# Storing a pooling state in contiguous rows after a copy on the chip, in a hybrid decoder step

## The chip, the core and the metric

The kernel runs on one core of a Trainium2 chip, as one program. The metric is device time in microseconds: the median of three runs. The core has five engines that run side by side and wait for one another through semaphores: PE (matrix products), DVE (VectorE), ACT (ScalarE), POOL (GpSimd) and SP (SyncE, which here only issues transfers). ACT and POOL can issue transfers too. In the profile, "SPq" and "ACTq" are the issues of transfers by SP and ACT.

## What is computed

One inference step of two layers for a prompt of 1024 positions and a group of 8 samples that share the weights. Layer 0 mixes a multi-scale pooling branch with an RWKV-7 branch; layer 1 is a chunked gMLP. Each layer then has cross-attention into 256 memory tokens and a squared-ReLU MLP. What matters here is the state that the pooling branch hands on: for each sample, the last 15 of the rows (15 old ones, then the new one).

```python
def pool_mix(z, buf, pos0, w_group, scale):
    full = jnp.concatenate([buf.astype(z.dtype), z], axis=1)
...
    return y.astype(z.dtype), full[:, -POOL_BUF:]
```

`buf` is `state_pool`, 8 samples x 15 rows x 512 channels in float32; the second result is `pool_sample`, of the same shape. The kernel keeps channels in partitions (128 channels x 4 groups), so on the chip and in its output tensor `ps` the state is 128 rows of 480 numbers: 4 groups x 8 samples x 15 rows.

## The kernel before

**Arithmetic.** The large products are made in float32 from three products of a high and a low part. A weight unit (128 x 1024) is loaded by SP into one of two buffers `wr` (L204, in `wunit`), its high part is cast by ACT (L194), and its low part is formed by DVE or POOL (L195). PE then runs three products per block (L225, L226, L227, in `mm3`). A buffer `wr` can be loaded again when both parts of its earlier unit are made.

**Order.** The program is written once as straight code, and the build fixes an order of instructions for each engine and each issuing queue from its own estimate of when each is ready. This order is not the written one: in the profile SP issues L969 and L970, which are written after the loop over the four pooling groups, ahead of the third group's L967. On the chip each engine takes its list strictly in order, so an instruction that waits holds all that stand behind it on that engine.

**What runs around the change.** Around 375 us four pieces of work are interwoven by generators:
- `pooling()` (L931 to 972), four groups. For each: the last rows of the prompt and the new sample column are copied by POOL (L940, L941); windowed sums by doubling on POOL or DVE (L946, with small copies L947); the mean minus the token (L953 to L958); a 128 x 128 product (L965) whose result ACT scales (L966); and a store of the group's result into `mixd` by SP (L967). At the end the two pooling states are stored: the prompt's (`pp`, L969) and the samples' (`ps`, L970).
- `inverses(s)` (L893 to 914): DVE inverts small triangular blocks by a loop of L907 and L908; ACT makes a transposed copy (L911); SP stores both forms into `xid` (L912, L913).
- `indep` and `Chain` (L1117 to 1216): the chunked RWKV recurrence. For each segment ACT issues the loads of `prd` (L1124), `xid` (L1130, L1131), `abd` (L1135) and `vd` (L1137), PE works on them (L1145, L1154), and then a serial chain of small products follows (L1178 to L1212).
- `memkv` (L1025 to 1058): keys and values of the memory tokens, unit by unit from `in_wk` and `in_wv`, used to fill PE's time between the chain's steps. For each unit of keys, DVE scales the product (L1032) and SP stores it to the output `mk` (L1033).

**The names of the edit.** `pbuf` is one 128-partition buffer. Its first 512 columns, viewed as `pb4`, hold for 4 groups and 8 samples 16 entries each: the 15 old rows and the new one. Columns 512 to 991 are `pin`, into which the old state is loaded (L928), contiguous; POOL spreads it from there into `pb4` (L929), and `pin` is not read again. The state that is stored is `pb4[..., 1:16]`: 15 numbers, one left out, 15 numbers, and so on.

Of the kernel before, what the change touches and what calls it, by code (L numbers as in the profile page):

```python
# [125 lines left out]
def hybrid_step(ctx: ExitStack, tc: tile.TileContext, I, O):  # L126
    nc = tc.nc
    te, ve, se, po, sy = nc.tensor, nc.vector, nc.scalar, nc.gpsimd, nc.sync
# [13 lines left out]
    def get(dt=F32):  # L142
        i = free.popleft()
        t = sb.tile([128, T], dt, tag=f"s{i}", name=nm("s"))
        owner[id(t)] = (i, t)
        return t

    def put(*ts):
        for t in ts:
            free.append(owner.pop(id(t))[0])  # L150

    def small(shape, tag, bufs=2, dt=F32):
        return sb.tile(shape, dt, tag=tag, bufs=bufs, name=nm(tag))
# [20 lines left out]
    def psm():  # L174
        return cyc("m", ("in0", "in1", "c0b", "c1b") if wide[0] else ("in0", "in1"))
# [11 lines left out]
    def pc(name, i):  # L187
        c = PCOL[name] + i
        return par[:, c : c + 1]
# [463 lines left out]
    def bulk(n=1):  # L653
        for _ in range(n):
            next(zs_, None)
            if side and next(side[0], 0) == 0:
                side.popleft()
# [268 lines left out]
    pb4 = pbuf[:, 0:512].rearrange("p (g b t) -> p g b t", g=4, b=8)  # L926
    pin = pbuf[:, 512:992]
# [3 lines left out]
    def pooling():  # L931
        for g in range(4):
            zused[0] = zorder.index(g)
            while g not in zready:
                bulk()
                yield
            zused[0] += 1
            z = zready.pop(g)
            win = WIN[g]
            po.tensor_copy(out=ppo[:, g, :], in_=z[:, NP - 15 : NP])  # L940
            po.tensor_copy(out=pb4[:, g, :, 15:16].rearrange("p b t -> p (b t)"), in_=z[:, NP:T])  # L941
            cur, step = z, 1
            while step < win:
                nx = get()
                eng = (po, ve)[PG[{1: 0, 2: 4, 4: 8, 8: 12}[step] + g]]
                eng.tensor_tensor(out=nx[:, step:NP], in0=cur[:, step:NP], in1=cur[:, 0 : NP - step], op=ALU.add)  # L946
                po.tensor_copy(out=nx[:, 0:step], in_=cur[:, 0:step])  # L947
                if cur is not z:
                    put(cur)
                cur, step = nx, step * 2  # L950
            d = get()
            o = C1["cnt"][0] + 16 * g
            ve.scalar_tensor_tensor(out=d[:, 16:NP], in0=cur[:, 16:NP], scalar=1.0 / win, in1=z[:, 16:NP], op0=ALU.mult, op1=ALU.subtract)  # L953
            ve.tensor_tensor(out=cur[:, 0:16], in0=cur[:, 0:16], in1=c1[:, o : o + 16], op=ALU.mult)
            ve.tensor_tensor(out=d[:, 0:16], in0=cur[:, 0:16], in1=z[:, 0:16], op=ALU.subtract)
            t = small([128, 8], "pws")
            ve.tensor_reduce(out=t, in_=pb4[:, g, :, 16 - win : 16], axis=AX.X, op=ALU.add)
            ve.scalar_tensor_tensor(out=d[:, NP:T], in0=t, scalar=1.0 / win, in1=z[:, NP:T], op0=ALU.mult, op1=ALU.subtract)  # L958
            put(cur)
            bulk()  # L960
            for _ in range(PLY):
                yield
            for g0, g1 in GR:
                ps = psm()
                te.matmul(ps[:, : g1 - g0], g2t[:, 512 + g * 128 : 640 + g * 128], d[:, g0:g1], start=True, stop=True)  # L965
                se.activation(out=z[:, g0:g1], in_=ps[:, : g1 - g0], func=AF.Copy, scale=pc("psc", g))  # L966
            sy.dma_start(out=mixd[g], in_=z)  # L967
            put(z, d)
        sy.dma_start(out=O["pp"], in_=ppo)  # L969
        sy.dma_start(out=O["ps"].rearrange("p (n t) -> p n t", t=15), in_=pb4[:, :, :, 1:16].rearrange("p g b t -> p (g b) t"))  # L970
        put(pbuf, g2t, c1)
        yield

# [289 lines left out]

    segs = [[(0, n)] * (n < 4) + [(1, n - 1)] * (n > 0) for n in range(5)]
    pg = pooling()

    def start(n):
# [897 lines left out]
```

## Time and profile before

| | us |
|---|---|
| median of 3 runs (3176.22 to 3179.43) | 3179.05 |
| the profiled execution | 3185.59 |
| its span, first to last instruction | 3183.8 |
| POOL busy in it | 717.3 |
| store of `ps` (L970): issued at | 375.48 |
| store of `ps`: from issue to landing | 17.9 |
| store of `pp` (L969), 30 KB, contiguous rows: from issue to landing | 1.5 |

The profile is of one execution, and all times in it are counted from its span's start. A row of the timeline reads: start, duration, engine, line, operation, output<-inputs, shape, and in brackets the idle time of that engine just before and what ended it. A row of issues reads: what was moved, the issuing queue, how many, KB each, and the median time from issue to landing. A row of waits reads: who waited <- for whom: total us, times, the longest.

### The profile page before, as it was taken

What the parts mean: (1) busy time and instruction counts of PE and PEld (TensorE: products, weight loads), DVE (VectorE), ACT (ScalarE), POOL (GpSimd) and SP (SyncE); (2) the same over time, 40 slices, a digit from 0 to 9 for tenths busy, and PEclk for the clock granted to TensorE, in tenths of its full rate; (3) what the DMA queues carried; (4) which work ended last, traced back from release to release, by engine and by line L of the source; (5) the groups of instructions that cost most, each with busy time, mean ns of one, the idle gap of its engine ahead of it and who ended that gap; (6) DMA issues with size and microseconds to landing.
All of it is one profiled execution on the core that took longest, in us unless ns stands there. A gap on an engine that the chain in (4) does not pass through costs nothing. (4 is left out here: it accounts for less than half of the span.)

```text
span 3183.8 us, 59345 instructions
## 1 busy us (share of the span) xinstructions
PE 3081.0 (97%) x23514; PEld 2957.1 (93%) x23514; DVE 2086.6 (66%) x3778; ACT 1353.3 (43%) x2757; POOL 717.3 (23%) x650
## 2 busy tenths in 40 slices
PE   8999889999999999999999999999999999999998
PEld 7987778899899999999999999899989999999998
DVE  4688734644457887566787776656455788765775
ACT  5223234433345444544455454614334544453443
POOL 5233424320021223022131100223001122211213
PEclk9999989999999999999999999999999999999999
DMA  3346577643522444866522223524343244476643
GB/s 119 117 132 208 88 247 234 209 140 120 180 87 103 158 160 173 218 174 174 174 89 99 88 94 138 204 80 143 113 147 120 94 158 156 164 236 140 181 166 121
DMA packets 215846, 473.25 MB, mean 149 GB/s; under 512 B 47374, under 2 KB 72334, under 8 KB 215567
## 3 DMA queue, kind: packets, MB, share of 16 engines
q1 hardware_dynamic: 188814, 423.63, 39.0%
q0 software_dynamic: 6912, 25.37, 4.6%
q10 hardware_dynamic: 19840, 20.45, 2.3%
q8 instruction: 185, 3.03, 0.4%
q14 instruction: 95, 0.77, 0.1%
HBM read 309.87 MB, written 159.50 MB: 147 GB/s over the span
## 5 line engine op out<-in xcount | busy, mean ns | idle before, releaser
L454 PE MATMUL ps<-s,wp 128*128 128x258 f32 x3584 | 1018.7, 284 | 11.3 <-DVE s L490 5.9
L456 PE MATMUL ps<-s,wp 128*128 128x258 f32 x3584 | 1013.2, 283 | 4.4 <-DVE wp L195 4.2
L455 PE MATMUL ps<-s,wp 128*128 128x258 f32 x3584 | 1014.1, 283 | 0.0
L454 PEld LDWEIGHTS ps<-s,wp 128*128 128x128 f32 x3584 | 677.8, 189 | 15.2 <-DVE s L490 6.7
L456 PEld LDWEIGHTS ps<-s,wp 128*128 128x128 f32 x3584 | 678.9, 190 | 5.7 <-DVE wp L195 5.7
L455 PEld LDWEIGHTS ps<-s,wp 128*128 128x128 f32 x3584 | 680.5, 190 | 0.2 <-issue 0.2
L225 PE MATMUL ps<-s,wh 128*128 128x384 f32 (+2 forms) x1994 | 649.5, 327 | 19.3 <-ACT wh L194 16.5
L226 PE MATMUL ps<-s,wh 128*128 128x384 f32 (+2 forms) x1994 | 643.6, 323 | 0.1
L227 PE MATMUL ps<-s,wl 128*128 128x384 f32 (+2 forms) x1994 | 640.0, 322 | 0.4 <-DVE wl L195 0.4
L225 PEld LDWEIGHTS ps<-s,wh 128*128 128x128 f32 x1994 | 380.6, 191 | 30.4 <-ACT wh L194 17.3
L226 PEld LDWEIGHTS ps<-s,wh 128*128 128x128 f32 x1994 | 381.1, 191 | 7.9 <-issue 6.0
L227 PEld LDWEIGHTS ps<-s,wl 128*128 128x128 f32 x1994 | 380.0, 191 | 6.0 <-issue 4.1
L265 POOL TENSOR_TENSOR s<-s,m 128x384 f32<-128x384 f32 (+1 forms) x147 | 162.0, 1110 | 652.6 <-ACT m L264 651.7
L194 ACT CAST s<-s 128x516 fp32r<-128x516 f32 (+6 forms) x316 | 199.2, 657 | 144.2 <-DMA s<-hts 32.5
L195 DVE TENSOR_TENSOR wp<-wr,wp 128x512 fp32r<-128x512 f32 x200 | 159.9, 800 | 89.9 <-ACT wp L194 88.1
L194 ACT CAST wh<-wr 128x1024 fp32r<-128x1024 f32 x110 | 115.1, 1047 | 200.1 <-PE ps L226 155.1
L194 ACT CAST wp<-wr 128x512 fp32r<-128x512 f32 x200 | 124.5, 622 | 129.1 <-issue 48.3
L195 DVE TENSOR_TENSOR wl<-wr,wh 128x1024 fp32r<-128x1024 f32 x97 | 121.5, 1254 | 58.5 <-ACT wh L194 53.9
L195 DVE TENSOR_TENSOR s<-s,s 128x516 fp32r<-128x516 f32 (+6 forms) x148 | 122.5, 841 | 52.2 <-ACT s L194 40.5
L225 PE MATMUL ps<-s,s 128*128 128x384 f32 (+3 forms) x432 | 142.9, 333 | 6.9 <-ACT s L1768 6.5
L195 DVE TENSOR_TENSOR s<-s 128x516 fp32r<-128x516 f32 x168 | 116.3, 726 | 37.5 <-ACT s L194 37.0
L226 PE MATMUL ps<-s,s 128*128 128x384 f32 (+3 forms) x432 | 139.6, 323 | 0.0
(346 smaller groups left out, 5271.3 us busy)
## 6 DMA issues: line engine op xcount, KB each, us to landing
hdn<-s SPq DMA_DIRECT2D x128, 258.0 KB, 2.1
hts<-s SPq DMA_DIRECT2D x48, 516.0 KB, 2.7
s<-hts SPq DMA_DIRECT2D x96, 258.0 KB, 6.6
xf<-s POOLq DMA_DIRECT2D x48, 516.0 KB, 7.5
s<-hdn SPq DMA_DIRECT2D x72, 258.0 KB, 5.4
s<-in_wd SPq DMA_DIRECT2D x34, 512.0 KB, 5.2
s<-in_kc SPq DMA_DIRECT2D x64, 256.0 KB, 3.6
s<-in_vc SPq DMA_DIRECT2D x64, 256.0 KB, 3.1
```

The source lines that it names most:

```text
L194: se.copy(out=hi, in_=src)
L195: (eng or ve).tensor_tensor(out=lo, in0=src, in1=f(hi), op=ALU.subtract)
L225: te.matmul(out, wh, xh, start=i == 0, stop=False)
L226: te.matmul(out, wh, xl, start=False, stop=False)
L227: te.matmul(out, wl, xh, start=False, stop=i == n - 1)
L265: po.tensor_tensor(out=self.acc[:, g0:g1], in0=self.acc[:, g0:g1], in1=sq, op=ALU.add)
L454: te.matmul(out, wh, xh, start=j < 4 and k == 0, stop=False, skip_group_check=j >= 4)
L455: te.matmul(out, wh, xl, start=False, stop=False, skip_group_check=j >= 4)
L456: te.matmul(out, wl, xh, start=False, stop=k == 3, skip_group_check=j >= 4)
```

## The change

After the four groups, POOL copies the 480 state numbers of each partition from `pb4` (runs of 15 with one left out) into `pin`, where they lie side by side, and SP stores `pin` to the output as 128 rows of 1920 bytes. Before, SP stored straight from `pb4`, in runs of 15 numbers (60 bytes). The bytes written to the output are the same. POOL gets one instruction more, and SP's store now waits for it.

```diff
         sy.dma_start(out=O["pp"], in_=ppo)
-        sy.dma_start(out=O["ps"].rearrange("p (n t) -> p n t", t=15), in_=pb4[:, :, :, 1:16].rearrange("p g b t -> p (g b) t"))
+        po.tensor_copy(out=pin.rearrange("p (n t) -> p n t", t=15), in_=pb4[:, :, :, 1:16].rearrange("p g b t -> p (g b) t"))
+        sy.dma_start(out=O["ps"], in_=pin)
         put(pbuf, g2t, c1)
```

## The prediction

> **What bounds the kernel now.** I read the page's first part, then PE busy time by stretch around the edited line, then what PE and SyncE waited for there, then the timelines of the five engines, and last the landing times of the transfers.
>
> ```profile
> span 3183.8 us, 59345 instructions
> PE 3081.0 (97%) x23514; PEld 2957.1 (93%) x23514; DVE 2086.6 (66%) x3778; ACT 1353.3 (43%) x2757; POOL 717.3 (23%) x650
> ```
>
> PE is busy 3081.0 of 3183.8 us. A transfer can only matter if it is behind part of the 102.8 us in which PE is not. The edited store is issued at 375.48 us, so the stretches after it come next (columns: PE, PEld, DVE, ACT, POOL busy us and instructions, granted clock, DMA share, GB/s).
>
> ```profile
> 381.00:385.00 4.00, 0.00 (x0) 0.00 (x0) 4.00 (x8) 0.10 (x1) 3.56 (x4) 0.50 2.05 26
> 385.00:391.00 6.00, 5.87 (x19) 4.69 (x20) 5.58 (x16) 0.00 (x0) 1.61 (x3) 0.50 1.33 68
> 395.00:405.60 10.60, 0.00 (x0) 0.00 (x0) 0.00 (x0) 3.92 (x4) 0.00 (x0) 0.65 0.74 247
> 405.60:411.80 6.20, 6.15 (x26) 5.74 (x26) 1.56 (x2) 1.53 (x2) 0.00 (x0) 0.50 1.06 396
> ...
> PE ps L225 <- ACT wh L194: 12.4, 2, 10.9
> ...
> SPq L204 <- DMA out_mk<-m: 14.0, 1, 14.0
> ```
>
> Two holes in PE's work, 381 to 385 and 395 to 405.6, each followed by some 6 us at a granted clock of 0.50. In the first hole DVE is busy all of 4.00 us: that hole is DVE's. In the second, DVE and POOL do nothing and ACT 3.92 us: nobody computes. Its last releaser for PE is the cast of a weight unit (L194), and the weight load behind that (L204) stood 14.0 us on SyncE until a 128 KB result store, out_mk, had landed. Now the chain itself, SyncE first, then the engines.
>
> ```profile
> 375.48 0.57 SPq L970 DMA_DIRECT2D out_ps<-s  x1
> 377.11 6.14 SPq L967 DMA_DIRECT2D mixd<-s  x1
> 383.34 0.56 SPq L1033 DMA_DIRECT2D out_mk<-m  x1
> 398.00 0.33 SPq L204 DMA_DIRECT2D wr<-in_wk  x1
> ...
> 400.95 0.32 SPq L913 DMA_DIRECT2D xid<-s  x1
> ...
> 380.80 12.96 ACTq L1131 DMA_DIRECT2D s<-xid  x4
> ...
> 399.01 1.92 ACT L911 COPY s<-s 128x1024 f32<-128x1024 f32 x1
> ...
> 404.55 1.04 ACT L194 CAST wh<-wr 128x1024 fp32r<-128x1024 f32 x1 [3.15 <-DMA wr<-in_wk]
> ...
> 409.48 0.36 ACTq L1131 DMA_DIRECT2D s<-xid  x1
> ...
> 394.33 0.28 PE L226 MATMUL ps<-s,wh 128*128 128x256 f32 x1
> 394.44 0.28 PE L227 MATMUL ps<-s,wl 128*128 128x256 f32 x1
> 405.65 0.58 PE L225 MATMUL ps<-s,wh 128*128 128x256 f32 x1 [10.93 <-ACT wh L194]
> ...
> 411.88 0.64 PE L1145 MATMUL ps<-s,s 128*32 128x32 f32 x28
> ```
>
> The issue of the mixd store takes 6.14 us and that of four small xid loads 12.96 us, where the issue of the weight load at 398.00 takes 0.33. Both queues are choked from 377 to 394 us. What chokes them is in the DMA view: first the edited store, then the same kinds of transfers over the whole span, then those issued from 376 to 394 us, with that window's two queues.
>
> ```profile
> out_ps<-s SPq DMA_DIRECT2D x1, 240.0 KB, 17.9
> out_wks<-s SPq DMA_DIRECT2D x4, 256.0 KB, 2.5
> wr<-in_wk SPq DMA_DIRECT2D x16, 512.0 KB, 5.6
> s<-prd ACTq DMA_DIRECT2D x16, 512.0 KB, 4.7
> out_mk<-m SPq DMA_DIRECT2D x16, 128.0 KB, 6.2
> ...
> q1 hardware_dynamic: 4192, 0.31, 104.8%
> q10 hardware_dynamic: 496, 0.96, 44.2%
> s<-prd ACTq DMA_DIRECT2D x2, 512.0 KB, 18.0
> s<-xid ACTq DMA_DIRECT2D x4, 32.0 KB, 16.0
> out_mk<-m SPq DMA_DIRECT2D x1, 128.0 KB, 14.6
> ```
>
> The edited store moves 128 rows of 32 runs of 15 floats: 4096 runs of 60 bytes, 245,760 bytes. The window's SyncE queue (q1) shows 4192 packets for 0.31 MB, so nearly all are those runs. It lands after 17.9 us, at 393.4; the neighbours that were issued behind it take 14.6 to 18.0 us, those of ACT's queue (q10) included.
>
> **The change, part by part.** *The store.* It becomes 128 runs of 1920 bytes. The nearest row is out_wks: 256 KB from 128 contiguous rows of 2048 bytes, 2.5 us. I take 2.5 for 17.9, so 15.4 us of choked queues go. By itself that gives PE nothing; its worth is what it frees.
>
> What is late next, in order. The weight load (L204, call its unit U3) reuses the buffer of the unit before last, free when DVE has made that unit's low part:
>
> ```profile
> 385.77 1.22 DVE L195 TENSOR_TENSOR wl<-wr,wh 128x1024 fp32r<-128x1024 f32 x1
> ...
> 388.14 0.18 DVE L908 TENSOR_TENSOR s<-s,s 128x31 f32<-128x31 f32 x1
> ...
> xid<-s SPq DMA_DIRECT2D x2, 512.0 KB, 8.5
> ```
>
> DVE is in unbroken work there (4.00 of 4.00 and 5.58 of 6.00 us above), so 386.99 stays. The mixd store's issue, unchoked, ends near 377.5 instead of 383.25, so out_mk goes out between 377.5 and 383.3; I take 380 and its median of 6.2, which is before 387. (From 383.3 it would be 389.5, and U3 some 2.5 us later.) U3's load goes out at 387.0 instead of 398.0, lands 5.6 later (its median) at 392.6, is cast in 1.04 and is ready at 393.7; PE gets to it at 394.44 + 0.28 = 394.7. **The 10.93 us hole is gone**. Without it the 24 matmuls of U3 and the two of L965 do not run at half clock: 6.20 us of that stretch against 24 x 0.12 (the like matmuls at 394.33 and 394.44 start 0.11 apart, 0.12 with rounding) + 0.6 = 3.5, another **2.7**. Taken alone the two give 13.6 us, and that is the upper bound.
>
> PE then stands at 398.2 before L1145, which needs the second set of inverted blocks (xid), written by SyncE and read back by ACT. DVE finishes them at 388.32 (L908); ACT's copy (L911, 1.92) is now free to start then, as ACT no longer stands in its choked issues: 390.2. The xid store follows at 390.3. In the profile these stores took 8.5 us, in stretches at 247 and 396 GB/s; I keep that, since U3's load and ACT's abd loads (512 KB each) will move at the same time: 398.8. From the first xid load of ACT after it (409.48) to L1145 (411.88) are 2.4 us: **L1145 at 401.2 instead of 411.88, 10.7 us earlier.** So of 13.6 us, 3.0 go to a new wait.
>
> *The added copy.* The reverse of this copy, same shape, is L929:
>
> ```profile
> L929 POOL COPY s<-s x1: 583/583/583, 288.6 to 288.6; 128x480 f32<-128x480 f32 x1
> ...
> 375.11 2.86 POOL L946 TENSOR_TENSOR s<-s 128x1023 f32<-128x1023 f32 x1
> ...
> 380.76 0.94 POOL L1120 MEMSET s<- 64x1024 f32 x1 [2.54 <-PE ps L1212]
> ...
> 379.86 1.21 DVE L946 TENSOR_TENSOR s<-s 128x1022 f32<-128x1022 f32 x1
> ...
> 391.08 1.04 POOL L1226 TENSOR_TENSOR s<-s,gnq 128x512 f32<-128x512 f32 x1 [1.56 <-DVE gnq L1225]
> 424.14 1.65 POOL L1231 TENSOR_TENSOR gnq<-gnq,mhalf 128x8 f32<-128x8 f32 x1 [32.01 <-DVE gnq L1230]
> ```
>
> 0.58 us, in POOL's 2.54 us of idleness before 380.76: cost nothing. If it goes ahead of POOL's L946 instead, that addition and its small copies end 0.58 after 378.2, and DVE, which needs them at 379.86, has 1.6 us to spare: nothing again. It may be slower beside DVE (POOL's own L946 takes 2.86 us for what DVE does in 1.21); even three microseconds still leave it done by 382.
>
> *The added wait.* The store now waits for POOL, so it moves on SyncE from 375.48 to about 379. Behind it stand the mixd store, out_mk and U3's load. The first is read much later, and U3's load is not due before 387.0. Between 379 and 387 the wait costs nothing.
>
> *Carrying to the end.* After 411.8 the order on every engine is fixed, and what PE waits for is released by earlier work that has moved too (10.9 of the 12.4 us that it waits for L194 up to 600 us are this hole), so I carry the 10.7 us whole. The ends here are all of it, and half, should a later load be no earlier; I take the whole, as no row shows such a load.
>
> **Sum.** 3185.59 (profiled execution: 3183.8 of span and 1.8 around it) - 10.7 = 3174.9. That execution is 6.5 us above the median of 3179.05; on the median's scale the forecast is **3168.4**. If the whole 6.5 us were this burst, swollen by the recording, 4.2 us would be left: 3174.9, inside the range.
>
> **The rivals.**
>
> *The new gap halves the clock (3171.4).* The wait I foresee before L1145 is 3.0 us. The hole of 4.0 us and more was followed by half clock for 6 us (385 to 391, 0.50). If 3.0 does the same, 6 us of work take as long as 3 us would, and 3.0 of the 10.7 go back: 7.7 gained. For it: the hole lies close. Against: the landing I took is the slow one. The Trainium skill, "TensorE: Matmul & The Clock Gate", Why this matters for your kernels, asks for no PE gaps over about 3 us, since one idle window brings half rate; the rows at 385 and 405.6 agree with that for 4.0 and 10.9 us, and none here lies at 3.
>
> *ACT's loads are slow by themselves (3179).* The xid loads read short pieces too. If they and the prd loads choke ACT until 394 without the store, L911 stays near 399, L1145 near 411.9, and PE waits there instead: gain 0. For it: ACT's queue has the larger bytes (0.96 MB against 0.31). Against: prd loads land in 4.7 us elsewhere, and the mixd issue, choked too, is SyncE's. A rule of the skill speaks for this rival: "DMA: Bandwidth & Descriptors", Queues, rings and completion order, has each DMA engine take turns between the queues, packet by packet, so that ACT's loads should not have stood behind SyncE's store, and by it the time would be this rival's 3179. The trace is against it in this stretch: 496 packets got through on ACT's queue while 4192 did on SyncE's.
>
> *Part of it (3174.5).* The loads come earlier but collide: U3's load, two abd loads, two xid stores and the next unit's load are 3 MB within 10 us. If the xid store takes 10 us, L1145 starts at 390.3 + 10 + 2.4 = 402.7, 9.2 earlier, and if half of that is kept, 4.6 us are gained. For it: 3 MB in 10 us are 300 GB/s, not far from the 396 at most in the stretches above. Against it: no row shows a later stage that waits for these loads.
>
> *Slower: SyncE stands behind POOL (3207).* The order on each engine is fixed when the program is built. If the copy comes after L1226 and after L1231, which waits for DVE until 424.14, the store holds SyncE until 426.4 and U3's load goes out 28 us later than now: 3179 + 28. It decides from 398.0 on: a copy that ends before then holds back nothing that was not held back already. After L1226 alone it would end at 392.7 and still win some. Against it: the copy is ready at 375.15, long before L1231's inputs.
>
> *The change does not do what it says.* Should the store still go out in short runs, all stays and the copy is added: 3179. I count it with no change; out_wks shows that contiguous rows land fast.
>
> **How the numbers follow.** Forecast 0.45, half clock 0.13, part 0.20, no change 0.15, slower 0.07. A measurement of this kernel tells about 0.2% (6.4 us) from no change. The forecast and the half clock lie beyond that, and half of the part case (where over 0.7 of the 9.2 us is kept): 0.68 faster. The other half with no change: 0.25. The predicted time is the forecast's, 3168.4. The range runs from 3163 (the upper bound of 13.6 and the 0.1% by which runs differ) to 3179, which takes in the part case and half of the no-change case.
>
> **What would show it.** Right: out_ps lands in 2 to 4 us, prd and xid loads behind it in about 5; U3's load goes out near 387; PE's 10.9 us wait for L194 is gone; L1145 starts near 401, with a wait of 1 to 4 us before it; PE busy time falls by about 3 us and the rest of the gain is idle time. Wrong: ACT still takes over 10 us to issue four xid loads; the copy stands after 398 on POOL; or L1145 comes near 401 and the span does not follow, which would be a later stage that gives it back.

## The result, and the profile after

The changed kernel took 3161.43 us (median of 4 runs, 3160.59 to 3167.70) beside 3179.24 us for the kernel before (4 runs, three of them the runs of the table above): a ratio of 0.9944, 95% interval 0.9928 to 0.9959, or 17.8 us. The forecast was 3168.4, the range 3163 to 3179. The sign was right; the time lies 1.6 us below the range. Two later comparisons gave the changed kernel less: 3162.10 beside 3174.14 (0.9960, 0.9946 to 0.9975) and 3165.01 beside 3176.42 (0.9968, 0.9955 to 0.9980). How these fit together is the main question below.

The order of instructions on every engine is the same in both programs, but for the copy on POOL; lines from 971 on stand one lower in the changed kernel. Its page begins with

```profile
span 3165.9 us, 59346 instructions
```

and in the stretch that answers to 381 to 420 us of before, its busy time is (columns as before)

```profile
379.60:383.60 4.00, 0.00 (x0) 0.00 (x0) 4.00 (x8) 0.12 (x1) 3.58 (x4) 0.91 0.93 308
383.60:389.60 6.00, 5.85 (x19) 4.67 (x20) 5.59 (x17) 3.09 (x3) 1.62 (x3) 0.50 0.83 271
393.30:396.50 3.20, 3.20 (x28) 3.00 (x27) 0.43 (x2) 0.48 (x1) 0.00 (x0) 1.00 0.97 337
396.50:405.70 9.20, 8.33 (x96) 7.72 (x95) 3.30 (x4) 2.82 (x4) 0.00 (x0) 1.00 0.94 258
```

DVE's hole (379.6 to 383.6) and the half clock after it are as they were. The second hole and its half clock are not there: U3's matmuls run from 393.3 to 396.5 at clock 1.00. The timelines of the changed kernel, SP, then POOL, ACT and PE:

```profile
377.23 0.34 SPq L971 DMA_DIRECT2D out_ps<-s  x1
377.67 0.38 SPq L967 DMA_DIRECT2D mixd<-s  x1
378.14 0.45 SPq L1034 DMA_DIRECT2D out_mk<-m  x1
385.63 0.34 SPq L204 DMA_DIRECT2D wr<-in_wk  x1
...
389.03 0.32 SPq L913 DMA_DIRECT2D xid<-s  x1
...
376.54 0.67 POOL L970 COPY s<-s 128x480 f32<-128x480 f32 x1
...
379.41 2.93 ACTq L1132 DMA_DIRECT2D s<-xid  x4
...
391.02 1.05 ACT L194 CAST wh<-wr 128x1024 fp32r<-128x1024 f32 x1 [1.53 <-DMA wr<-in_wk]
...
395.31 0.36 ACTq L1132 DMA_DIRECT2D s<-xid  x1
...
396.26 0.28 PE L227 MATMUL ps<-s,wl 128*128 128x256 f32 x1
396.47 0.64 PE L1146 MATMUL ps<-s,s 128*32 128x32 f32 x28
397.97 0.39 PE L225 MATMUL ps<-s,wh 128*128 128x256 f32 x1 [0.87 <-ACT wh L194]
```

The mixd store is issued in 0.38 us instead of 6.14, ACT's four xid loads in 2.93 instead of 12.96. U3's load goes out at 385.63, not 398.00. PE goes from U3's last product (396.26) straight into the recurrence (L1146, L1145 of before), which started at 411.88. In the DMA view of 376 to 392 us the transfers behind the store land as elsewhere:

```profile
s<-prd ACTq DMA_DIRECT2D x2, 512.0 KB, 4.4
...
out_ps<-s SPq DMA_DIRECT2D x1, 240.0 KB, 4.8
s<-xid ACTq DMA_DIRECT2D x4, 32.0 KB, 3.5
```

The store takes 4.8 us instead of 17.9; the prd loads took 18.0 and the xid loads 16.0.

### The profile page after: what moved, and what is told of

The parts are those of the page before. It is cut to its first block, busy times and chain, and to the rows that moved or that the text cites. A ratio compares the mean times of both kernels' runs of the same rounds, so it can differ in the third digit from the quotient of the medians.

```text
span 3165.9 us, 59346 instructions
## 1 busy us (share of the span) xinstructions
PE 3075.7 (97%) x23514; PEld 2951.2 (93%) x23514; DVE 2090.0 (66%) x3778; ACT 1353.3 (43%) x2757; POOL 716.2 (23%) x651
## 5 line engine op out<-in xcount | busy, mean ns | idle before, releaser
L195 DVE TENSOR_TENSOR wp<-wr,wp 128x512 fp32r<-128x512 f32 x200 | 159.2, 796 | 85.1 <-ACT wp L194 82.5
L195 DVE TENSOR_TENSOR s<-s,s 128x516 fp32r<-128x516 f32 (+6 forms) x148 | 121.7, 835 | 53.3 <-ACT s L194 46.5
L195 DVE TENSOR_TENSOR wl<-wr,wh 128x1024 fp32r<-128x1024 f32 x97 | 122.9, 1268 | 47.8 <-ACT wh L194 42.9
L195 DVE TENSOR_TENSOR s<-s 128x516 fp32r<-128x516 f32 x168 | 116.6, 728 | 43.6 <-ACT s L194 41.8
```

What stands on the lines that cost most here:

```text
L195: (eng or ve).tensor_tensor(out=lo, in0=src, in1=f(hi), op=ALU.subtract)
```

## Experiments

All kernels but the last and the one that issues from ACT keep the order of before on every engine, apart from the added copy or the altered store. Each comparison is with runs of the kernel before on the same chip.

**Is it the copy? (copy_alone)**

```diff
+        po.tensor_copy(out=pin..., in_=pb4[:, :, :, 1:16]...)
         sy.dma_start(out=O["ps"].rearrange("p (n t) -> p n t", t=15), in_=pb4[:, :, :, 1:16]...)
```

> The copy is made on POOL, but the store still goes out from the old place in 4096 runs of 60 bytes; the copied rows are not used. Theory (the short runs are the whole matter): the time of before, 3179 within 4 us; the hole of about 10.9 us before the weight unit at 405 stays, the store lands after about 18 us. Rival (a part of the gain is the new instruction's, through POOL's times or places): 3 us or more faster than before.

3177.32 us beside 3174.14, ratio 1.0004 (0.9992 to 1.0016). The store lands after 15.8 us, and PE's wait is there:

```profile
PE ps L225 <- ACT wh L194: 10.1, 1, 10.1
```

The copy alone does nothing for the time that can be told. The gain is the form of the store.

**Does the copy, or its wait, cost anything? (rows16, rows16_again, after_pitch512)** The 16-wide rows are contiguous without any copy, if one row in 16 too many is stored:

```diff
-        sy.dma_start(out=O["ps"].rearrange("p (n t) -> p n t", t=15), in_=pb4[:, :, :, 1:16]...)
+        sy.dma_start(out=O["ps"], in_=pbuf[:, 0:512])
...
-    "ps": (128, 480)
+    "ps": (128, 512)
```

> No copy and no added wait: the whole 16-wide rows of the buffer, 2048 contiguous bytes per partition, are stored straight away, one row of 16 too many, which is dropped where the result is unpacked. Theory (copy and wait cost nothing): the time of the changed kernel, 3161 within 3 us. Rival (the copy or the wait behind POOL costs something): 3 us or more faster than the changed kernel.

3167.41 us, ratio 0.9979 (0.9970 to 0.9988): 5 us above the changed kernel's second median on the same chip, against either expectation. Its store landed after 2.0 us. So it was run again, with a third kernel that keeps the copy but has the 512-column output:

```diff
-        sy.dma_start(out=O["ps"], in_=pin)
+        sy.dma_start(out=O["ps"][:, 0:480], in_=pin)
...
-    "ps": (128, 480)
+    "ps": (128, 512)
```

> The rows of 16 again. In the stretch behind the edit it gained as much as the changed kernel did, yet its median was 5 us higher. Theory (drift between runs): within 2 us of the changed kernel. Rival (it is slower by something outside the stretch): 4 to 6 us above the changed kernel again.

> The changed kernel with an output tensor of 512 columns, of which 480 are written, so that the outputs lie in memory as they do with the rows of 16. If the rows of 16 are slower again, theory (where the output tensors lie in memory makes it): this one is slower than the changed kernel by 4 to 6 us as well. Rival (the missing copy or the missing wait makes it): this one is within 2 us of the changed kernel.

3163.28 us (0.9962, 0.9950 to 0.9975) and 3162.55 (0.9962, 0.9949 to 0.9976), beside 3165.01 for the changed kernel. The three are within each other's intervals: the 5 us did not come back, and neither the copy nor the place of the outputs has a price that can be told. The premise of the third expectation was thus not met.

**What is left to win from this store? (no_store)** The diff takes the line out.

> The sample group's pooling state is neither copied nor stored; its output is left out. This bounds what any form of this store can bring. Theory: 3161 within 3 us, as the contiguous store lies beside other work. Rival (240 KB more on the queues still push the loads behind them): 3 us or more faster than the changed kernel.

3163.61 us, ratio 0.9961 (0.9940 to 0.9981), six runs from 3151.95 to 3168.77. That is the changed kernel's time as far as six such runs can tell (the interval is 13 us wide). The stretch behind the edit, measured below, says it more sharply: 22.5 us without the store, 21.9 to 24.4 in the changed kernel. Nothing that can be told is left.

**How does the loss grow with the number of short runs? (runs2048, runs3072)** With k = 2 and k = 1:

```diff
-        sy.dma_start(out=O["ps"].rearrange(...), in_=pb4[:, :, :, 1:16]...)
+        sy.dma_start(out=O["ps"][:, 120 * k : 480].rearrange(...), in_=pb4[:, k:4, :, 1:16]...)
```

> Only the last two of the four groups are stored, straight from the old place, in 2048 runs of 60 bytes; half of the sample group's pooling state is left out. At 17.9 us for 4096 runs the store lands after about 9 us, near 384.5. Theory (the choke costs only from the point at which the weight load's buffer is free, 387.0): nearly the whole gain, 13 to 17 us below before, 3162 to 3166. Rival (each run costs its share of the gain): half of it, about 9 us, 3170.

> Only the last three of the four groups are stored, in 3072 runs of 60 bytes; a quarter of the sample group's pooling state is left out. The store lands after about 13.4 us, near 389. Theory (cost only from 387.0 on, and with it the half clock): the weight load near 393.5 instead of 398.0, 4 to 6 us below before, 3173 to 3175. Rival (each run its share): 4.5 us, 3174.7. The two agree here; with the run of 2048 it shows whether the curve has a bend.

Half the runs: 3168.38 us beside 3176.20 (0.9980, 0.9969 to 0.9992), 7.8 us. Three quarters: 3176.36 (0.9995, 0.9984 to 1.0006), no gain that can be told; the 4 to 6 us and 4.5 us expected of it reach into the far end of that interval (5.1 us). The stores landed after 9.9 and 13.4 us. SP's waits say what I had left out; first half the runs, then three quarters:

```profile
SPq L204 <- DMA out_mk<-m: 9.7, 1, 9.7
```

```profile
SPq L204 <- DMA out_mk<-m: 13.1, 1, 13.1
```

U3's load follows not the store, but the out_mk store that landed about 4 us after it (388.3 with 2048 runs, whose store landed at 384.4). PE's hole before U3 is 4.1 and 6.9 us there. In the stretch from the pooling products to L1154, measured in the next but one experiment, the kernel with 2048 runs takes 26.1 us, with 3072 29.7, with 4096 33.7 (mean of three) and without the store 22.5. So the first 2048 runs cost 3.6 us, the second 7.5. That hints at a bend and does not show one: there is one profile for each smaller count, and executions of one kernel lie up to 2.5 us apart in this stretch. My figure of 13 to 17 us for half the runs was wrong; the rival's 9 was nearer.

**Is it the queue or the engines behind it? (from_act)**

```diff
-        sy.dma_start(out=O["ps"].rearrange(...), in_=...)
+        se.dma_start(out=O["ps"].rearrange(...), in_=...)
```

> The old store of 4096 runs of 60 bytes, issued by ACT instead of SP, so that it lies in the other queue; some matrix products after 405 us change places on PE with it. Theory (the runs jam the 16 engines for both queues, as ACT's loads stood behind SP's store before): SP's out_mk store and weight load are late again by 5 us or more, and the time is within 5 us of before. Rival (the engines take turns between the queues packet by packet): SP's mixd store is issued in under 1 us, out_mk lands in under 7 us and the weight load goes out before 390, while ACT's four xid loads still take over 10 us to issue; part of the gain, 3165 to 3174.

3184.24 us, ratio 1.0028 (1.0015 to 1.0041), 8 us slower, where the theory had it within 5. The issues on SP, then on ACT, then its DMA view of 374 to 394 us, and then PE's waits from 376 to 420 us:

```profile
374.53 0.32 SPq L967 DMA_DIRECT2D mixd<-s  x1
376.64 0.34 SPq L1033 DMA_DIRECT2D out_mk<-m  x1
393.58 0.33 SPq L204 DMA_DIRECT2D wr<-in_wk  x1
...
374.67 0.64 ACTq L970 DMA_DIRECT2D out_ps<-s  x1
375.41 6.87 ACTq L1124 DMA_DIRECT2D s<-prd  x1
```

```profile
q10 hardware_dynamic: 4382, 1.06, 111.5%
q1 hardware_dynamic: 288, 0.66, 22.4%
...
mixd<-s SPq DMA_DIRECT2D x1, 516.0 KB, 3.5
...
out_mk<-m SPq DMA_DIRECT2D x1, 128.0 KB, 16.9
s<-xid ACTq DMA_DIRECT2D x4, 32.0 KB, 13.5
```

```profile
PE ps L225 <- ACT wh L194: 9.9, 2, 9.5
```

The short runs now lie on ACT's queue (q10), and SP's (q1) holds the mixd store and out_mk. The mixd store landed after 3.5 us and says nothing about the jam: here it was issued 0.14 us ahead of the short runs, not behind them. out_mk was issued 2 us after them. Its issue took 0.34 us, but it landed after 16.9 us all the same, U3's load goes out at 393.58, and PE has its hole of 9.5 us. The two parts of the rival came apart: this issue on SP was not held, but the transfer stood still. So the jam is not in one queue; it is in what both queues share. Whether that is the DMA engines themselves or the memory behind them, no run here tells. (The Trainium skill, "DMA: Bandwidth & Descriptors", Queues, rings and completion order, has the engines take turns between queues by packet. The trace agrees in so far as both queues moved in the same stretch: from 380 to 392 us 144 packets of SP's queue and 1583 of ACT's. But all of it was slow, 0.72 MB in those 12 us, so that taking turns did not spare out_mk the wait.) Why this kernel is slower than before by 8 us is not settled: its stretch to L1154 is 31.7 us, no longer than before's, so in the profiled execution the time is lost later. The order on PE is another in this kernel, which may be the reason; no run tests it.

**Where do the rest of the 17.8 us come from? (before_again, after_again, after_third)** The same two kernels, profiled again.

> The kernel before once more, for a second profile. Theory: the hole of 10 to 12 us before the weight unit is there again, at 394 to 406 us; the rest of the span drifts by up to 2 us against the first profile. Rival (the hole is an accident of the one profiled execution): under 5 us of it.

> The changed kernel once more, for a second profile. Of the 17.9 us between the two profiled spans, 1.4 lie before the edited line, 14.0 in the stretch behind it, and some 2.5 after 412 us. Theory (only the 14.0 belong to the change by mechanism, the rest drifts from run to run): the part before the edit is again anything from -1.5 to 1.5, and the part after 412 us moves by 2 us or more between the two profiles. Rival (the later stages gain 2 to 4 us of their own): the part after 412 us is again 2 to 4 us.

> The changed kernel a third time, beside the rows of 16 and many runs of the kernel before on one chip. Of 18 us in the first comparison and 12 us in the second, about 11 to 13 are seen in the stretch behind the edit. Theory (that stretch is all that the change does): 11 to 14 us below before. Rival (later stages gain some 4 us too, as the first comparison had it): 15 to 18 us below.

From PE's timelines I take three marks: the last group's first pooling product (L965, behind DVE's hole), the first product of the next recurrence segment (L1145) and the first L1154 after it. The rows for the first executions, before and then after:

```profile
385.13 2.90 PE L965 MATMUL ps<-s,s 128*128 128x384 f32 x4 [4.43 <-DVE s L953]
...
420.19 0.38 PE L1154 MATMUL ps<-s,s 128*32 128x32 f32 x12
```

```profile
383.75 2.90 PE L965 MATMUL ps<-s,s 128*128 128x384 f32 x4 [4.44 <-DVE s L953]
...
405.70 0.38 PE L1155 MATMUL ps<-s,s 128*32 128x32 f32 x12
```

| execution | start to L965 | L965 to L1145 | L1145 to L1154 | L1154 to the end | span |
|---|---|---|---|---|---|
| before | 385.1 | 26.8 | 8.3 | 2763.6 | 3183.8 |
| before_again | 380.2 | 24.8 | 8.3 | 2756.7 | 3170.0 |
| copy_alone | 380.8 | 24.6 | 8.3 | 2754.6 | 3168.3 |
| mean with 4096 runs | 382.0 | 25.4 | 8.3 | 2758.3 | 3174.0 |
| after | 383.8 | 12.7 | 9.2 | 2760.2 | 3165.9 |
| after_again | 379.3 | 11.7 | 11.2 | 2757.0 | 3159.1 |
| after_third | 380.9 | 11.9 | 12.5 | 2757.9 | 3163.2 |
| mean of the changed kernel | 381.3 | 12.1 | 11.0 | 2758.4 | 3162.7 |

The first column is before the edit, the fourth far behind it: each moves by 3 to 9 us among the three executions of a group, and its means do not differ by more than 0.7 us between the groups. In the two middle columns the kernels are apart by 13.3 - 2.7 = 10.6 us. That is what the change does in this stretch. Three more executions with contiguous rows (rows16, rows16_again, after_pitch512) have 22.8, 25.7 and 24.0 us in the two middle columns together, and 2760.4, 2752.6 and 2751.8 us behind them; with them the kernels are 10.0 us apart in the middle and 1.7 us behind it. The other 7 of the 17.8 us I put down to drift. For the first comparison by itself this is argued, not shown: its interval is 13 to 23 us, and a later gain of 1 or 2 us is not ruled out. The median of before in the first comparison, 3179.24 of 4 runs, lies above the later ones (3174.14 of 22 runs, 3176.20 of 31, 3176.42 of 9). Those 62 runs reach from 3168.25 to 3182.29, 0.4%. The hole is no accident: 10.9, 10.4 and 10.1 us in the three. The 2 us of drift that I expected between two profiles of the kernel before were far too few: 4.9 ahead of the edit and 6.9 far behind it. The 11 to 14 us expected of the third comparison came as 11.4.

**The wait that is left (mk_from_pool)**

```diff
-            sy.dma_start(out=O["mk"][l, m], in_=o[:, 0:256])
+            po.dma_start(out=O["mk"][l, m], in_=o[:, 0:256])
```

> The changed kernel, with the 16 stores of out_mk issued by POOL instead of SP; some products and evacuations after 390 us change places with it. In the changed kernel PE waits 0.9 to 2.8 us for the cast of the unit after U3, whose load stands on SP behind an out_mk store. Theory (that store's place holds the load): the load goes out some 2 us earlier, the wait falls under 1 us, and the time is 1 to 4 us below the changed kernel (3163). Rival (the load's own transfer among the others is what is late, or the new order costs more): the wait stays at 2 us or more, the time is the same or higher.

3167.01 us beside 3175.79, ratio 0.9976 (0.9965 to 0.9987): no better than the change alone. The next load goes out at 388.35, 5.7 us after L965 starts, where the three executions of the changed kernel have 6.7 to 7.8; that is 1.0 to 2.1 us earlier. Yet PE's wait from 370 to 410 us is

```profile
PE ps L225 <- ACT wh L194: 2.3, 1, 2.3
```

This wait stands ahead of L1146, as the order on PE is another here. The load took 8.6 us to land, where it took 5.3 to 7.4 in the changed kernel: what was gained at its issue was lost in its transfer. No version beat the changed kernel by more than its interval.

## Why the prediction was right, and where it was wrong

**The bound, right.** The second hole was the short store's, by the chain that was read: out_mk, U3's load, its cast. Taking the short runs away in three other ways (rows16, no store, another output pitch) took the hole away too.

**The store, right in effect.** 4.8 us where 2.5 were taken. Without the copy it was 2.0, but there the store went out ahead of the mixd store and the prd loads, and with the copy right among them.

**U3, right to 0.2 us.** Shifted by the 1.4 us that this execution was ahead at L965, the forecast's 387.0 for the load and 393.7 for the cast's end are 385.6 and 392.3; they were 385.63 and 392.07. The load went out when DVE had made the low part of the earlier unit (L195, 384.38 to 385.60), as forecast; out_mk had landed some 2 us before. The half clock over U3 went as well: 3.2 us for 3.5.

**The new wait, wrong in place, and right in size by luck.** The forecast had 13.6 us freed and 3.0 lost before L1145. L1145 waited for nothing and started at 396.47, where the shifted forecast is 399.8: the xid store landed 6.3 us after its issue (389.03 to 395.31, when ACT's load follows), not the 8.5 that I kept. But 2.7 us are lost behind L1145, around the next weight unit (waits of 0.9, 2.8 and 2.6 us in the three executions). Net 10.6 us for the 10.7 of the forecast; nothing in its working led to this second loss, and that it is about as large as the one foreseen is luck.

**The copy and its wait, right.** The copy took 0.67 us on POOL, directly behind L946, in idle time; SP's store waited 3.5 us, and nothing behind it was late.

**Carrying to the end, right as far as the table tells.** The last column's means are 0.1 us apart, with executions 3 to 9 us apart.

**The range, wrong.** The step that failed is its lower end, "the upper bound of 13.6 and the 0.1% by which runs differ", with the base of 3179.05 from which it was counted. Both came from three runs. The 62 later runs of the same kernel spread over 0.4%, their medians lie 2.6 to 4.9 us under that base, and the mean of the three profiled spans with short runs is 9.8 us under the one that I worked from. In the first pair of profiles the two middle columns differ by 13.1 us, still inside the upper bound, and the two outer ones by another 4.8, for which the range had left some 2.5. The first result, 17.8 us, is 1.7 times the forecast mostly for that reason; no mechanism that was missed shows in the table.

**The rivals.** ACT's loads being slow by themselves fell: they land in 3.5 and 4.4 us, and with it fell the 3179 worked out from packets taking turns. The collision (part of it) fell: the xid store took 6.3 to 7.1 us in the three executions, not 10. The store went out as the change says: it landed in under 5 us. SP behind POOL fell: the copy stood right behind the addition. That the new gap halves the clock came true in some executions, at another place: see below.

## What to carry to other kernels

When PE stands still with every engine idle, follow the load it waits for back through its queue to the transfer that landed last before its issue, and look at what was in flight then, on all queues: one small store of many short runs can hold 0.5 MB loads for its whole length (18.0 us here). A copy on an idle engine that makes the rows contiguous is worth it where the store runs ahead of loads that have less slack than the store is long; the price is to be read at the load's due time, not from the store's length. And before a range for a few tenths of a per cent is drawn, the spread of the unchanged kernel has to be known from more than three runs.

## What the runs showed of the hardware

4096 runs of 60 bytes took 15.5 to 17.9 us to land, 128 rows of 1920 bytes 4.4 to 4.9, and 128 rows of 2048 bytes, issued ahead of the prd loads, 2.0. A jam of short runs on one queue holds the other: out_mk took 16.9 us with the short runs on ACT's queue and 12.8 to 14.6 with them on its own. The runs are not moved evenly: the profile of before lists 2388 packets on SP's queue from 376.3 to 379.2 us, at some 100 GB/s for the first two of them, and 1737 in the 14.8 us after that. With 2048 runs, 2064 packets under 512 bytes are listed from 375.4 to 378.0, and the store lands only at 384.4. So a store of short runs lands long after most of its runs are listed as moved; what it waits for in the end is not shown.

Gaps of 2 to 3 us on PE sometimes halve its clock and sometimes don't. The stretch before and after the gap behind L1145, for after_again and then for after_third and rows16_again:

```profile
391.00:394.40 3.40, 0.62 (x29) 0.51 (x28) 0.43 (x2) 1.52 (x2) 0.00 (x0) 1.00 0.92 307
394.40:398.00 3.60, 3.58 (x32) 3.22 (x33) 2.45 (x2) 1.77 (x3) 0.00 (x0) 1.00 0.70 176
```

```profile
392.80:396.10 3.30, 0.69 (x30) 0.52 (x28) 0.44 (x2) 1.53 (x2) 0.00 (x0) 1.00 0.88 292
396.10:400.00 3.90, 3.89 (x25) 3.48 (x26) 2.44 (x2) 1.77 (x3) 0.00 (x0) 0.68 0.76 158
```

```profile
393.80:396.80 3.00, 0.69 (x30) 0.52 (x28) 0.44 (x2) 1.53 (x2) 0.00 (x0) 0.97 0.82 264
396.80:400.00 3.20, 3.19 (x19) 2.57 (x19) 2.44 (x2) 1.77 (x3) 0.00 (x0) 0.50 0.69 165
400.00:407.00 7.00, 7.00 (x47) 7.00 (x47) 0.42 (x1) 2.05 (x3) 0.00 (x0) 0.75 0.99 288
```

PE is busy 0.6 to 0.7 of some 3 us in all three. The clock stays whole in the first, and falls to 0.68 and 0.50 in the others. The stretch from L1145 to L1154 grows with it, from 11.2 us to 12.5 and 13.5. The Trainium skill, "TensorE: Matmul & The Clock Gate", Part 1, has the gate watch windows of about 3.4 us that run freely, whatever the program does; that the clock is halved in some executions and not in others agrees with that. That a gap of 2.3 us, shorter than a window, is enough, while the longest of the three, 2.8 us, left the clock whole, no run here explains.
